# Attention's second pass three steps ahead at a change of head, and its products two steps behind in the projection

## The chip, the cores and the metric

The kernel runs on one core of a Trainium2 chip. The metric is the device time of one execution in microseconds (us): 2467.56 is the median of three runs of the kernel before (2466.41 to 2468.1). The engines are TensorE (PE, with its weight loads as PEld), VectorE (DVE), ScalarE (ACT), GpSimd (POOL) and SyncE (SP); transfers are issued from SP's and POOL's queues.

## The reference

One layer works on x of 2048 tokens by 1024 columns. A normed input is projected by w_in; three mixers share the result; their outputs are projected by w_out and added; then comes a feed-forward of 4096 hidden columns, and a last norm.

```python
def _layer(x, ...):
    p = _rmsnorm(x, g_attn) @ w_in
    # mixer a: y_a = a_b * conv3(a_c * a_h)
    # mixer b: GLU, causal conv of width 31, layer norm, silu
    # mixer c: stick-breaking attention, 8 heads of 64:
        z = q @ k.T / sqrt(64)
        mask = s_idx < t_idx
        log_beta = log_sigmoid(z)
        log_1m = where(mask, log_beta - z, 0.0)
        suffix = cumsum(log_1m, reverse=True) - log_1m
        a = where(mask, exp(log_beta + suffix), 0.0)
        o = a @ v
    x = x + concat([y_a, y_b, y_c]) @ w_out
    return x + square(relu(_rmsnorm(x, g_ffn) @ w_ff1)) @ w_ff2
```

The weight a of a key is its own sigmoid times the product of (1 - sigmoid) over the keys behind it up to the query. The kernel computes these products directly, with sigmoids and multiplications, from the last key to the first.

## The kernel before

All large products are made of three: each operand is split into a high and a low part, and hi x hi, lo x hi and hi x lo are summed (L103, L105, L107 in one helper). A split is a copy on ScalarE (L88, the high part) and a subtraction (L90, the low part) on VectorE or GpSimd.

The program has two stages. In the **projection** (to about 515 us), `p_half` makes tiles ps_p of 128 x 512, each of 24 products. Beside it, as side generators, run the mixers (mixer b is 30 multiply-adds on VectorE per tile, L450), the splitting of weights for later (`pre_split`), and attention for the first quarter of the queries. Then come four **blocks** of 512 tokens (`block(tb)`, tb = 0 to 3). Each makes the out-projection (ps_x2 in the program's text, ps_x in the profile), the first feed-forward product (ps_u, then ScalarE and VectorE make fh and fl, L899) and the second (ps_y, added to acc at L924). Their weights come as w<-s_w_out and w<-s_w over SP's queue. Attention for quarters 1, 2 and 3 of the queries runs beside blocks 0, 1 and 2.

Attention goes in 32 groups (h, i): head h, quarter i, in the order i = 0 with heads 0 to 7, then i = 1 and so on. They are called heads 0 to 31 here. A group does this:

- `a_load`: the queries and the keys of its own quarter into KQd, two transfers on POOL's queue. KQd has one buffer, so the load can't start before the last product that reads it, of the head ahead.
- `a_pass1`: 3 + 4i steps. Each makes one tile ps_z of logits (L513, L514), sigmoids A and om or R, and the running products (A*R on GpSimd L593, R on VectorE L595). Steps 0 to 2 treat the diagonal part, the others the earlier keys Kl, which are loaded behind KQd.
- `a_cross_a`: the running product across the partitions, on VectorE: a transpose to T (L606), a scan to O (L609), the factors C (L617) and T again (L623). It is made twice where i > 0, once after step 2 and once at the end.
- `a_pass2`: 3 + 4i steps. Each multiplies A by ps_q (the factors transposed, L641; L644 for the first three steps, L651 for the others), splits it (Ahi at L88 on ScalarE, Alo at L90 on GpSimd) and makes the products with the values into ps_o (L682 for the first three steps with Vd, L690 and L691 for the others with Vl). The products of a step are issued a few steps later, as the entry `late` says.

`attention` runs pass 1 of one head and pass 2 of the head ahead in alternation, by counting the steps done, d1 of n1 and d2 of n2. The load for the next head is placed after both are through. A side generator is advanced by `weave`: it is to have done so much of its cost when the main work has come so far. The sizes of the buffer rings stand in `self.ab`, one for the projection (pool at1), one for the blocks (pool at2).

The order on each engine is not that of the text alone: the framework's scheduler, with its own simulated time, arranges the instructions. What each engine has in its list stands fixed from then on, and it works it off in order.

Of the kernel before, what the change touches and what calls it, by code (L numbers as in the profile page):

```python
# [68 lines left out]
class Trunk:  # L69
# [195 lines left out]
    def norm_spread(self, g):  # L265
        self.R[g] = self.mx.tile([P, TB], F32, name="R", tag="Rs", bufs=4)
        self.nc.scalar.activation(self.R[g], self.spread(self.rv[g], "o" if g else "q"), AF.Copy)

# [54 lines left out]
    def p_evac(self, hf, u, sub, tb, ps):  # L323
# [4 lines left out]
        kind = UNITS[u]  # L328
        R = self.R[gtb]
        sig, ca = self.sig, self.ca  # L330
# [206 lines left out]
    def a_pass1(self, g):  # L537
        nc, pool, i = self.nc, self.at, g["i"]
        ab = self.ab
        lo, hi2 = slice(0, 256), slice(256, 512)  # L540

        def new(name, bufs, shape=(P, TB), dt=F32):
            return pool.tile(list(shape), dt, name=name, tag=name, bufs=bufs)

        if i:
            g["Kl"] = pool.tile([P, self.kmax], F32R, name="Kl", tag="Kl", bufs=self.ab["Kl"])
            for rows, kq in self.kq_halves(g["h"]):
                to = g["Kl"][rows, : TB * i].rearrange("c (j q) -> c j q", j=2)
                self.load_r(to, kq[:, 0, :, : TB * i // 2])
        A0 = g["A0"] = []  # L550
        Rd = new("Rd", 1)

        k2 = [g["Kd"][:, 0:P], g["Kd"][:, 256 : 256 + P]]
        z = self.a_z(g, [(k2[1], lo, lo), (k2[0], lo, hi2)])
        t, om = self.a_diag(z, 0)
        nc.gpsimd.tensor_tensor(t[:, hi2], t[:, hi2], om[:, lo], op=ALU.mult)
        nc.vector.tensor_tensor(Rd[:, lo], om[:, lo], om[:, hi2], op=ALU.mult)
        A0.append(t)
        yield 1

        k4 = self.every(g["Kd"], 4)
        z = self.a_z(g, [(k4[3], hi2, lo), (k4[2], hi2, hi2)])
        t, om = self.a_diag(z, 1)
        nc.gpsimd.tensor_tensor(t[:, hi2], t[:, hi2], om[:, lo], op=ALU.mult)
        R = new("R", 2)
        nc.vector.tensor_tensor(R[:, lo], om[:, lo], om[:, hi2], op=ALU.mult)
        A0.append(t)
        yield 1
        z = self.a_z(g, [(k4[1], hi2, lo), (k4[0], hi2, hi2)])
        t, om = self.a_diag(z, 2)  # L570
        nc.vector.tensor_tensor(R[:, hi2], om[:, lo], R[:, lo], op=ALU.mult)
        nc.gpsimd.tensor_tensor(t, t, R, op=ALU.mult)
        nc.vector.tensor_tensor(Rd[:, hi2], om[:, hi2], R[:, hi2], op=ALU.mult)
        A0.append(t)
        yield 1
        tot = self.a_cross_a(g, Rd, None)
        if not i:
            return
        J = 4 * i
        kl = self.every(g["Kl"][:, : TB * i], J)  # L580
        full = slice(0, TB)
        R = None
        for j in range(J - 1, -1, -1):
            z = self.a_z(g, [(kl[j], full, full)])
            t = new("A0", ab["A0"])
            if R is None:
                nc.scalar.activation(t, z, AF.Sigmoid, scale=0.125)
                R = new("R", 2)
                nc.scalar.activation(R, z, AF.Sigmoid, scale=-0.125)
            else:  # L590
                nc.scalar.activation(t, z, AF.Sigmoid, scale=0.125)  # L591
                nc.scalar.activation(z, z, AF.Sigmoid, scale=-0.125)  # L592
                nc.gpsimd.tensor_tensor(t, t, R, op=ALU.mult)  # L593
                Rn = new("R", 2)
                nc.vector.tensor_tensor(Rn, z, R, op=ALU.mult)  # L595
                R = Rn
            A0.append(t)
            yield 1
        self.a_cross_a(g, R, tot)
# [93 lines left out]
    def attention(self, groups):  # L693
        prev = None
        nxt = self.a_load(*groups[0])
        for n in range(len(groups) + 1):
            g, nxt = nxt, None
            p1 = self.a_pass1(g) if g else iter(())
            p2 = self.a_pass2(prev) if prev else iter(())
            n1 = 3 + 4 * g["i"] if g else 0  # L700
            n2 = 3 + 4 * prev["i"] if prev else 0
            d1 = d2 = 0.0
            live1, live2 = g is not None, prev is not None
            loaded = False
            while live1 or live2:
                if live2 and (not live1 or d2 * max(n1, 1) <= d1 * max(n2, 1)):
                    try:
                        next(p2)
                        d2 += 1
                        yield 0.5  # L710
                    except StopIteration:
                        live2 = False
                elif live1:
                    try:
                        next(p1)
                        d1 += 1
                        yield 0.5
                    except StopIteration:
                        live1 = False
                if not loaded and self.ab["KQd"] > 1 and d1 >= n1 / 2 and n + 1 < len(groups):  # L720
                    nxt = self.a_load(*groups[n + 1])
                    loaded = True
            if not loaded and n + 1 < len(groups):
                nxt = self.a_load(*groups[n + 1])
            prev = g
# [269 lines left out]
    def build(self):  # L995
        tc = self.tc
        with ExitStack() as ctx:
            self.consts(ctx)
            self.attention_consts(ctx)
            self.raw = ctx.enter_context(tc.tile_pool(name="raw", bufs=1))  # L1000
            self.xb = 5
            self.presplit = [("w_out", c, q) for c in range(DC) for q in range(2)] + [("w1", c, q) for c in range(PRE) for q in range(2)]
            self.g, self.u, self.w, self.R, self.rv, self.sig, self.ca, self.ss, self.yraw = ({} for _ in range(9))
            with ExitStack() as c1:
                self.psum_pool(c1, d=3, c=1, z=2, q=1, o=1)
                self.p_pools(c1)
                self.w_eng = "dve"
                self.sb = 2
                self.xl = [[None] * DC for _ in range(2)]
                self.xh = [[None] * DC for _ in range(2)]  # L1010
                with tc.tile_pool(name="raw0", bufs=1) as self.rp:
                    self.rb, self.rt = 21, "raw"
                    self.p_start()
                self.rp = self.raw
                self.rb, self.rt = self.xb, "xt"
                self.at = c1.enter_context(tc.tile_pool(name="at1", bufs=1))
                self.ab = dict(KQd=1, Kl=1, A0=5, om=2, Alo=2, Ahi=2, Vl=1, late=1, yc=2)
                weave(self.p_half(0), [(Side(self.mixer_b(0)), 83, 20, 225, True), (Side(self.x_norms()), 24, 60, 180, True)])
                self.heads = {}
                a0 = Side(self.attention([(h, 0) for h in range(H)]))  # L1020
                weave(self.p_half(1), [(Side(self.mixer_b(1)), 90, 0, 190, True), (a0, 28, 0, 210, True), (Side(self.pre_split()), len(self.presplit), 0, 200, True)])
            with ExitStack() as c2:
                self.psum_pool(c2, d=3, z=3, q=1, o=1)
                self.at = c2.enter_context(tc.tile_pool(name="at2", bufs=1, reuse_waits="tile"))
                self.st = c2.enter_context(tc.tile_pool(name="st2", bufs=1, reuse_waits="tile"))
                self.ha = c2.enter_context(tc.tile_pool(name="ha", bufs=1, reuse_waits="tile"))
                self.hp = c2.enter_context(tc.tile_pool(name="hp", bufs=1, reuse_waits="tile"))
                self.ob = 2
                self.kmax = 1536
                self.ab = dict(KQd=1, Kl=1, A0=15, om=2, Alo=3, Ahi=3, Vl=2, late=2, yc=1)  # L1030
                at = Side(self.attention([(h, i) for i in (1, 2, 3) for h in range(H)]))
                self.heads = {}

                def attend(i):
                    while self.heads.get(i, 0) < H:
                        at.advance(at.done + 1)

                self.attend = attend
                self.end = iter(())
                for tb in range(4):  # L1040
                    weave(self.block(tb, self.end), [(at, (74, 95, 107)[tb], 45, 365 if tb < 2 else 320, False)] if tb < 3 else [])
# [48 lines left out]
```

## Time and profile before

| | us |
|---|---|
| median of three runs | 2467.56 (2466.41 to 2468.1) |
| profiled execution | 2472.6 |
| its span | 2470.9 |
| mean granted clock of TensorE | 0.988 |
| TensorE busy | 2399.2 (97%) |
| VectorE busy | 1605.9 (65%) |
| GpSimd busy | 1135.1 (46%) |
| ScalarE busy | 1033.8 (42%) |

The times come from runs without a profile; the profile is one execution more. A row of the timeline gives the start, the duration, the engine, line and operation, out<-in with the count, and in brackets how long the engine was idle ahead of it and what released it. A row of waits gives who waited for whom: the total, how often, the longest. The clock is the share of full speed that TensorE was granted.

### The profile page before, as it was taken

The numbers are of one execution on the slowest core, as the hardware profiler recorded it, in microseconds if no ns is written. First come the engines' busy times: TensorE is split into PE (matmuls) and PEld (weight loads), VectorE is DVE, ScalarE is ACT, GpSimd is POOL, SyncE is SP. The second block draws the span as 40 slices with busy tenths as digits, with TensorE's granted clock in tenths as the row PEclk, the third lists the DMA queues.
The fourth block names the chain that finished last, engine by engine and source line by source line (L and its number), as shares of the span: only waits on it lengthen the run. The fifth ranks groups of instructions, "written<-read, shape, count | busy, mean of one in ns | idle before, by whom it ended". The sixth has DMA issues, their size and how long they took to land.

```text
span 2470.9 us, 32483 instructions
## 1 busy us (share of the span) xinstructions
PE 2399.2 (97%) x11316; PEld 2017.4 (82%) x11316; DVE 1605.9 (65%) x2372; ACT 1033.8 (42%) x1910; POOL 1135.1 (46%) x1197
## 2 busy tenths in 40 slices
PE   8999989997999999999999999999999999999998
PEld 7888878896778878778888888888888888888887
DVE  7958698934688878867677768676666735212114
ACT  5233432223556656535455555345555532121121
POOL 1343246633376666635566667257888730000000
PEclk9999999998999999999999999999999999999999
DMA  7579997766778987787787777776666655655555
GB/s 260 191 263 305 303 299 188 233 204 221 214 208 238 224 242 208 183 236 262 252 228 249 234 230 210 238 243 178 188 195 198 199 191 203 245 194 187 202 181 188
DMA packets 237156, 550.62 MB, mean 223 GB/s; under 512 B 26048, under 2 KB 99776, under 8 KB 218560
## 3 DMA queue, kind: packets, MB, share of 16 engines
q1 hardware_dynamic: 180912, 474.07, 56.3%
q0 software_dynamic: 53888, 73.42, 15.6%
q8 instruction: 90, 1.47, 0.2%
q10 hardware_dynamic: 2192, 1.05, 0.1%
q14 instruction: 74, 0.61, 0.1%
HBM read 391.17 MB, written 148.90 MB: 219 GB/s over the span
## 4 chain that ended last, share of the span: by engine, by line
PE 74%; DVE 12%; DMA 9%; issue 3%; POOL 1%; ACT 1%; SPq 0%; POOLq 0%; DVEq 0%; ACTq 0%
PE ps_y L103 8%; PE ps_y L107 8%; PE ps_y L105 8%; PE ps_u L103 8%; PE ps_u L105 8%; PE ps_u L107 8%; PE ps_p L105 3%; PE ps_p L103 3%; PE ps_p L107 3%; DMA KQd<-KQ 2%; PE ps_z L513 2%; DMA w<-s_w 2%; PE ps_z L514 2%; PE ps_x L105 2%; DVE ps_c L450 2%
## 5 line engine op out<-in xcount | busy, mean ns | idle before, releaser
L90 POOL TENSOR_TENSOR Alo<-A,Ahi 128x512 fp32r<-128x512 f32 x288 | 398.8, 1397 | 112.1 <-ACT Ahi L88 44.5
L924 DVE TENSOR_TENSOR acc<-acc,ps_y 128x512 f32<-128x512 f32 (+1 forms) x264 | 174.7, 665 | 179.6 <-PE ps_y L107 178.2
L103 PE MATMUL ps_y<-fh,w 128*128 128x512 f32 (+1 forms) x1056 | 283.3, 386 | 7.3 <-DVE acc L924 4.3
L103 PE MATMUL ps_u<-hh,w 128*128 128x512 f32 x1024 | 277.6, 392 | 6.1 <-DMA w<-s_w 6.1
L105 PE MATMUL ps_y<-fh,w 128*128 128x512 f32 (+1 forms) x1056 | 279.5, 384 | 0.0
L107 PE MATMUL ps_y<-fl,w 128*128 128x512 f32 (+1 forms) x1056 | 278.7, 384 | 0.2 <-DVE fl L899 0.2
L107 PE MATMUL ps_u<-hl,w 128*128 128x512 f32 x1024 | 276.1, 390 | 0.0
L105 PE MATMUL ps_u<-hh,w 128*128 128x512 f32 x1024 | 275.3, 390 | 0.0
L593 POOL TENSOR_TENSOR A<-A,R 128x512 f32<-128x512 f32 x168 | 230.9, 1377 | 93.2 <-ACT A L591 73.5
L889 ACT ACTIVATE ps_u<-ps_u 128x512 f32<-128x512 f32 x128 | 74.6, 583 | 459.7 <-PE ps_u L107 459.6
L118 POOL TENSOR_TENSOR rs_y<-rs_v,mhalf 128x4 f32<-128x4 f32 (+1 forms) x13 | 14.3, 1097 | 513.1 <-DVE rs_v L117 453.6
L103 PEld LDWEIGHTS ps_y<-fh,w 128*128 128x128 f32 x1056 | 193.6, 188 | 46.6 <-DVE acc L924 3.8
L105 PEld LDWEIGHTS ps_y<-fh,w 128*128 128x128 f32 x1056 | 195.6, 189 | 40.1
L107 PEld LDWEIGHTS ps_y<-fl,w 128*128 128x128 f32 x1056 | 195.4, 188 | 39.8 <-DVE fl L899 0.6
L103 PEld LDWEIGHTS ps_u<-hh,w 128*128 128x128 f32 x1024 | 190.4, 188 | 45.3 <-DMA w<-s_w 8.0
L105 PEld LDWEIGHTS ps_u<-hh,w 128*128 128x128 f32 x1024 | 192.2, 188 | 40.7
L107 PEld LDWEIGHTS ps_u<-hl,w 128*128 128x128 f32 x1024 | 192.5, 188 | 40.0
L88 ACT ACTIVATE Ahi<-A 128x512 fp32r<-128x512 f32 x288 | 177.1, 629 | 97.3 <-PE ps_o L690 54.2
L899 DVE TENSOR_TENSOR fl<-ps_u,fh 128x512 fp32r<-128x512 f32 x128 | 87.6, 685 | 191.3 <-ACT fh L898 190.9
L595 DVE TENSOR_TENSOR R<-ps_z,R 128x512 f32<-128x512 f32 x168 | 115.4, 687 | 140.8 <-ACT ps_z L592 99.9
L450 DVE SCALAR_TENSOR_TENSOR ps_c<-g,wb,ps_c 128x512 f32<-128x512 f32 x240 | 179.9, 750 | 4.7
L90 DVE TENSOR_TENSOR w<-wraw,w 128x512 fp32r<-128x512 f32 x152 | 143.4, 962 | 36.1 <-ACT w L88 35.5
(171 smaller groups left out, 4850.5 us busy)
## 6 DMA issues: line engine op xcount, KB each, us to landing
w<-s_w SPq DMA_DIRECT2D x200, 512.0 KB, 3.5
w<-s_w SPq DMA_DIRECT2D x68, 1024.0 KB, 4.8
wraw<-in_w SPq DMA_DIRECT2D x192, 256.0 KB, 5.1
w<-s_w_out SPq DMA_DIRECT2D x64, 512.0 KB, 4.7
s_w<-w SPq DMA_DIRECT2D x32, 1024.0 KB, 6.0
s_w<-w SPq DMA_DIRECT2D x56, 512.0 KB, 4.9
KQd<-KQ POOLq DMA_DIRECT2D x64, 384.0 KB, 7.0
xraw<-in_xT SPq DMA_DIRECT2D x48, 256.0 KB, 4.8
```

The costliest lines, as they stand in the source:

```text
L88: nc.scalar.activation(hi, x, AF.Copy)
L90: e.tensor_tensor(lo, x, f(hi), op=ALU.subtract)
L103: self.nc.tensor.matmul(ps, wh, xh, start=start and k == 0, stop=False)
L105: self.nc.tensor.matmul(ps, wl, xh, start=False, stop=False)
L107: self.nc.tensor.matmul(ps, wh, xl, start=False, stop=stop and k == n - 1)
L450: nc.vector.scalar_tensor_tensor(t, g[:, k : k + TB], self.wb[:, c, k : k + 1], t, op0=ALU.mult, op1=ALU.add)
L513: nc.tensor.matmul(z[:, oc], keys, g["qh"][:, qc], start=k == 0, stop=False)
L593: nc.gpsimd.tensor_tensor(t, t, R, op=ALU.mult)
L595: nc.vector.tensor_tensor(Rn, z, R, op=ALU.mult)
L889: nc.scalar.activation(ps, ps, AF.Relu)
L899: nc.vector.tensor_tensor(lo, ps, f(hi), op=ALU.subtract)
L924: nc.vector.tensor_tensor(acc[d][:, cols], acc[d][:, cols], ps, op=ALU.add)
```

## The change

In the projection's `self.ab`, Alo and Ahi get three buffers instead of two, `late` is 2 instead of 1, and R has one buffer instead of two (a new entry, which only step 1 of pass 1 reads; the blocks keep two). In `attention`, pass 2 of the head ahead may go on while its steps less two are not ahead of pass 1's share, so that three of its steps instead of one come before the first step of pass 1. This holds only where the head ahead has i > 0; the others go as before.

```diff
-        R = new("R", 2)
+        R = new("R", ab["R"])
...
+            lead = 2 if prev and prev["i"] else 0
             loaded = False
             while live1 or live2:
-                if live2 and (not live1 or d2 * max(n1, 1) <= d1 * max(n2, 1)):
+                if live2 and (not live1 or (d2 - lead) * max(n1, 1) <= d1 * max(n2, 1)):
...
-                self.ab = dict(KQd=1, Kl=1, A0=5, om=2, Alo=2, Ahi=2, Vl=1, late=1, yc=2)
+                self.ab = dict(KQd=1, Kl=1, A0=5, om=2, R=1, Alo=3, Ahi=3, Vl=1, late=2, yc=2)
...
-                self.ab = dict(KQd=1, Kl=1, A0=15, om=2, Alo=3, Ahi=3, Vl=2, late=2, yc=1)
+                self.ab = dict(KQd=1, Kl=1, A0=15, om=2, R=2, Alo=3, Ahi=3, Vl=2, late=2, yc=1)
```

In the changed file the lines below `attention` have numbers higher by two.

The scheduler turns this into other orders. On TensorE in the projection, the four products of head 1's first pass-2 step (Vd_3005) stand among those of one ps_p tile. Before:

```order
L103 MATMUL ps_p<-xh_5_2462,wh_2785 128x512
L682 MATMUL ps_o<-Ahi,Vd_3005 128x256
L103 MATMUL ps_p<-xh_6_2468,wh_2785 128x512
L103 MATMUL ps_p<-xh_7_2474,wh_2785 128x512
L105 MATMUL ps_p<-xh_0_2432,wl_2784 128x512
L105 MATMUL ps_p<-xh_1_2438,wl_2784 128x512
L105 MATMUL ps_p<-xh_2_2444,wl_2784 128x512
L682 MATMUL ps_o<-Alo,Vd_3005 128x256
L682 MATMUL ps_o<-Ahi,Vd_3005 128x256
L682 MATMUL ps_o<-Alo,Vd_3005 128x256
```

And in the changed kernel, at the end of the same tile:

```order
L107 MATMUL ps_p<-xl_6_2469,wh_2781 128x512
L107 MATMUL ps_p<-xl_7_2475,wh_2781 128x512
L682 MATMUL ps_o<-Ahi,Vd_3005 128x256
L682 MATMUL ps_o<-Alo,Vd_3005 128x256
L682 MATMUL ps_o<-Ahi,Vd_3005 128x256
L682 MATMUL ps_o<-Alo,Vd_3005 128x256
L513 MATMUL ps_z<-KQd 128x256
```

The first of the four has moved behind 18 products of the tile, and all four stand together.

On VectorE in the out-projection of block 1 (acc is its sum, ss the sum of squares, ot the output of block 0), before:

```order
L793 TENSOR_TENSOR ss<-ss,sq 128x512
L595 TENSOR_TENSOR R<-ps_z,R 128x512
L606 STREAM_TRANSPOSE T<-R 128x16x32
L609 SCALAR_TENSOR_TENSOR O<-T,d_90 128x528
L617 TENSOR_TENSOR C<-C,O 32x16 x3
L623 TENSOR_TENSOR T<-O,C 128x16x32
L849 TENSOR_TENSOR acc_10428<-ps_x_10400,xt 128x512
L641 STREAM_TRANSPOSE ps_q<-T 128x512
L991 SCALAR_TENSOR_TENSOR ot<-acc_5674,g_final,ps_R 128x512
L651 TENSOR_TENSOR A_9912<-A_9912,ps_q 128x512
```

And now, at the same sum:

```order
L795 TENSOR_TENSOR ss<-ss,sq 128x512
L595 TENSOR_TENSOR R<-ps_z,R 128x512
L851 TENSOR_TENSOR acc_10426<-ps_x_10398,xt 128x512
L993 SCALAR_TENSOR_TENSOR ot<-acc_5674,g_final,ps_R 128x512
L857 SCALAR_TENSOR_TENSOR hl<-acc_10426,g_ffn,hh 128x512
L795 TENSOR_TENSOR ss<-ss,sq 128x512
L851 TENSOR_TENSOR acc_10469<-ps_x_10441,xt 128x512
```

The whole cross step of head 17 and the products with ps_q behind it have left the out-projection; they stand in the ps_u stage that follows.

On GpSimd, at the load of the keys of head 13 in block 0, before:

```order
L83 DMA Vd_7830<-VS 128x512
L90 TENSOR_TENSOR Alo<-A_7276,Ahi 128x512
L593 TENSOR_TENSOR A_7681<-A_7681,R 128x512
L90 TENSOR_TENSOR Alo<-A_7306,Ahi 128x512
L593 TENSOR_TENSOR A_7697<-A_7697,R 128x512
L83 DMA KQd<-KQ 64x6x256 x2
L83 DMA Kl<-KQ 64x2x256 x2
L90 TENSOR_TENSOR Alo<-A_7408,Ahi 128x512
L593 TENSOR_TENSOR A_7756<-A_7756,R 128x512
L83 DMA Vl<-VS 128x512
```

And now:

```order
L593 TENSOR_TENSOR A_7695<-A_7695,R 128x512
L90 TENSOR_TENSOR Alo<-A_7460,Ahi 128x512
L83 DMA Vl<-VS 128x512
L90 TENSOR_TENSOR Alo<-A_7512,Ahi 128x512
L90 TENSOR_TENSOR Alo<-A_7604,Ahi 128x512
L593 TENSOR_TENSOR A_7756<-A_7756,R 128x512
L83 DMA KQd<-KQ 64x6x256 x2
L83 DMA Kl<-KQ 64x2x256 x2
L593 TENSOR_TENSOR A_7808<-A_7808,R 128x512
L83 DMA Vd_8249<-VS 128x256
```

The load Vl of the values, which stood behind the keys, stands ahead of them, and the Vd for head 13's own second pass follow at once (those for head 12's, Vd_7830 among them, stand ahead in both orders).

## The prediction

> **What bounds the kernel now.** I read the page's first part, then the list of waits on TensorE, then the windows round its largest gaps, and last the timeline at the passages that the change moves.
>
> ```profile
> span 2470.9 us, 32483 instructions
> PE 2399.2 (97%) x11316; PEld 2017.4 (82%) x11316; DVE 1605.9 (65%) x2372; ACT 1033.8 (42%) x1910; POOL 1135.1 (46%) x1197
> ```
>
> TensorE is busy 2399.2 of 2470.9 us, and the change adds or removes no product. So the time can move only by the 71.7 us in which TensorE is idle, and by slow-clock time inside the busy part. The waits (total, times, longest) say where the idle time lies:
>
> ```profile
> PE ps_z L513 <- DMA KQd<-KQ: 13.6, 9, 2.9
> PE ps_x L103 <- ACT y L88: 9.1, 1, 9.1
> PE ps_o L682 <- ACT Ahi L88: 6.5, 2, 5.6
> PE ps_u L103 <- DMA w<-s_w: 6.1, 8, 1.9
> PE ps_y L103 <- DVE acc L924: 4.3, 4, 2.3
> PE ps_x L103 <- DVE A L651: 3.9, 1, 3.9
> PE ps_y L103 <- DVE fl L899: 2.9, 2, 2.2
> ```
>
> Three of them touch what the change moves: the one wait of a projection product on its split (L682, 5.6), the one in an out-projection (ps_x, 3.9) and the waits for a head's keys (KQd). The windows round them (the stretch and its length, busy time and instructions of TensorE, its weight loads, VectorE, ScalarE and GpSimd, then granted clock, DMA share, GB/s) show the clock:
>
> ```profile
> 316.00:384.00 68.00, 59.55 (x275) 49.29 (x276) 67.31 (x103) 21.60 (x42) 39.23 (x43) 0.95 0.87 293
> 327.00:342.00 15.00, 9.40 (x41) 7.60 (x40) 14.81 (x26) 5.52 (x13) 7.93 (x10) 0.77 0.76 283
> 900.00:920.00 20.00, 17.10 (x75) 13.94 (x74) 15.36 (x23) 11.04 (x21) 12.33 (x16) 0.91 1.25 293
> 1098.00:1112.00 14.00, 10.46 (x36) 8.45 (x37) 10.42 (x16) 5.49 (x10) 7.21 (x5) 0.76 0.79 262
> 1238.00:1250.00 12.00, 9.33 (x44) 7.96 (x44) 9.68 (x16) 4.99 (x10) 5.96 (x9) 0.86 1.00 260
> 1555.00:1612.00 57.00, 57.00 (x264) 47.60 (x263) 31.83 (x47) 20.25 (x35) 16.41 (x15) 1.00 0.81 265
> ```
>
> A gap is paid twice: 15 x (1 - 0.77) = 3.4 us round the 5.6 us gap and 14 x (1 - 0.76) = 3.4 us round the 3.9 us gap are lost to a lower clock, and 20 x 0.09 = 1.8 and 12 x 0.14 = 1.7 us round the two longest key waits.
>
> **A, two steps behind in the projection.** No instruction is added; the four products of Vd_3005 (head 1, k = 0) stand 18 projection products later. Eight such products take 1.81 us on the chain, so 18 x 0.227 = 4.1 us.
>
> ```profile
> 49.67 1.81 PE ps_p L103 x8
> 335.43 0.58 PE L682 MATMUL ps_o<-Ahi,Vd 128*128 128x256 f32 x1 [5.60 <-ACT Ahi L88]
> 345.29 1.67 POOL L361 TENSOR_TENSOR ca<-ca,R 128x512 f32<-128x512 f32 x1 [2.96 <-DVE ca L360]
> 346.91 1.36 POOL L83 DMA_DIRECT2D KQd<-KQ  x2
> 356.42 0.36 PE L513 MATMUL ps_z<-KQd 128*128 128x256 f32 x1 [2.07 <-issue]
> 394.11 0.35 PE L513 MATMUL ps_z<-KQd 128*128 128x256 f32 x1 [0.15 <-DMA KQd<-KQ]
> ```
>
> Most of 5.6 + 3.4 = 9.0 us vanishes at 335 us. But it is not the end of that account. VectorE is busy 67.31 of the 68 us from 316 to 384: that stretch is its work. The keys of head 3 are issued at 346.91 behind the mixer's L361 on GpSimd's queue, which waited for VectorE's L360; they come when VectorE lets them, and TensorE meets them at 356.42, where it waits already. What it saves at 335 it would wait again at 356 or at 394. I price A at 0. Upper bound: all of it kept, -9.0. Lower bound: a short wait at 356 or 394 grows by what is saved and far enough that the clock falls there too, as it did after the key wait in 1238 to 1250: +1.7. One buffer of R instead of two costs nothing: with i = 0 a head writes R once, and the next head's write comes a passage later (37 us between the two z rows above). The third Alo and Ahi make no instruction either; they only loosen GpSimd's L90.
>
> **B, the out-projection of block 1.** Before, the last z of head 17 and with it the load of head 18's keys fall in the ps_x stage:
>
> ```profile
> 1086.79 1.36 POOL L83 DMA_DIRECT2D KQd<-KQ  x2 [3.88 <-PE ps_o L682]
> 1088.14 1.21 POOL L83 DMA_DIRECT2D Kl<-KQ  x2
> 1091.57 0.32 SPq L79 DMA_DIRECT2D w<-s_w_out  x1
> 1101.54 1.19 PE L103 MATMUL ps_x<-y,w 128*128 128x512 f32 x2 [3.88 <-DVE A L651]
> ```
>
> The trace's name for this wait is VectorE's L651, but the weights asked for at 1091.57 had only landed at about 1101.4: the DMA view of 1086 to 1093 gives this load 9.8 us, the page 4.7 for all 64 of its kind.
>
> ```profile
> w<-s_w_out SPq DMA_DIRECT2D x3, 512.0 KB, 9.8
> KQd<-KQ POOLq DMA_DIRECT2D x2, 384.0 KB, 8.3
> Kl<-KQ POOLq DMA_DIRECT2D x2, 256.0 KB, 12.0
> w<-s_w_out SPq DMA_DIRECT2D x64, 512.0 KB, 4.7
> ```
>
> So about 2 x 384 + 2 x 256 + 256 KB of head loads went beside the weights. In the changed order two pass-2 steps come ahead of that last z, and since attention is advanced by the blocks' own progress, the last z falls behind the out-projection: between the sums of block 1 VectorE's order has no transpose, scan, C, or product with ps_q left, and GpSimd's no KQd. Block 2's out-projection, which has no passage, shows the result: 57.00 of 57.00 us busy (1555 to 1612). I take the whole 3.9 + 3.4 = -7.3; the other bound is 0, if the weights stay late for another cause.
>
> By the Trainium skill ("DMA: Bandwidth & Descriptors", Issuing engines are not separate DMA queues), transfers started by sync and by GpSimd end on the same 16 engines and interleave. The 9.8 against 4.7 us agrees; the rule speaks against the change as well, since the moved load is not gone but meets ffn1's weights (a rival below).
>
> **C, the passages in the blocks.** KQd has one buffer, so the load of a head's keys cannot be issued before the last z of the head ahead, and TensorE must fill the time till they land:
>
> ```profile
> DMA to landing us min/median/max: 4.5/7.0/13.4
> 900.90 9.90 DMA KQd<-KQ
> 910.93 0.36 PE L513 MATMUL ps_z<-KQd 128*128 128x256 f32 x1 [2.90 <-DMA KQd<-KQ]
> 1229.88 13.37 DMA KQd<-KQ
> 1243.38 0.55 PE L513 MATMUL ps_z<-KQd 128*128 128x256 f32 x1 [2.67 <-DMA KQd<-KQ]
> PE ps_z L513 <- DMA KQd<-KQ: 7.1, 5, 2.9
> PE ps_z L513 <- DMA KQd<-KQ: 2.7, 1, 2.7
> ```
>
> The last two rows are the list of waits cut to 600 to 1060 and to 1112 to 2060 us: 9.8 of the 13.6 us lie in the blocks.
>
> One would think that two more pass-2 steps ahead of the first z make this cover longer. Counted in both orders they do not. Over heads 9 to 31 (without 18 and 26) 46.8 products stand between last and first z before, 47.5 after: 46.8 x 0.227 = 10.6 and 10.8 us, because the two steps led are taken from the same place, behind the last z of the head ahead. Only the spread moves: head 11 goes from 9.5 to 14.0 us, head 13 from 11.1 to 7.9. Setting the time from last z to landing that each head had in this trace against the new covers gives 14.1 us of waits where the old covers give 9.8, and three slow-clock windows (3 x 1.7) for two: +6. But which load is slow depends on what runs beside it, and that moves too; by the equal mean alone it is 0. I take +3, the middle, as neither bound has a row nearer. The new pass-2 products need no load: the order puts Vd 25 to 40 rows of GpSimd ahead of them.
>
> The Trainium skill ("TensorE: Matmul & The Clock Gate", Part 1) has the clock halve only after an idle window of about 3.4 us. The rows differ: gaps of 2.67 and 2.90 us came with 0.86 and 0.91. By the page the clock's part of C would be nothing and its upper bound +4; I keep the rows.
>
> **D, VectorE's bursts in the blocks.**
>
> ```profile
> 996.28 7.68 DVE L609 TENSOR_TENSOR_SCAN O<-T,d 128x528 f32<-128x528 f32 x1
> 1012.20 0.96 PE L103 MATMUL ps_y<-fh,w 128*128 128x512 f32 x3 [2.27 <-DVE acc L924]
> 1710.17 1.64 PE L103 MATMUL ps_y<-fh,w 128*128 128x512 f32 x4 [2.23 <-DVE fl L899]
> ```
>
> At head 17 a scan of 7.68 us and the products with ps_q behind it hold up acc, and TensorE waits at 1012. The lead splits such bursts at some passages and joins them at others. The two rows' waits, with L924's 4.3 and L899's 2.9 in all and the clock's 1.7, bound it at about -4 and, mirrored, +4; I take -1.
>
> **Sum:** 0 - 7.3 + 3 - 1 = -5.3 us. The profiled execution took 2472.6 us with a span of 2470.9; it lies 5.0 above the median of the runs, 2467.56. So the profiled execution should come to 2467.3, and the median to 2467.56 - 5.3 = 2462.3; I say 2462.
>
> **The rivals.**
>
> Gain kept in the projection: VectorE's list between 316 and 384 us is not the bound all the way, and its order may put the mixer's row ahead of head 1's, so that the keys go out earlier. For it: GpSimd is busy only 39.23 of these 68 us, so it would issue them at once. Against it: VectorE's 67.31 of 68. Then -9.0 more: 2453.
>
> No change: B is gained, and the passages take it back by the +6 above and a burst of D in the wrong place (+1): 2467.56 - 7.3 + 7 = 2467.
>
> Slower, through one mechanism: GpSimd's queue in front of the keys. In the new order Vl's load stands four rows ahead of KQd where it stood behind it, and two Alo splits and a product A*R of the same size precede it, a split taking 1.4 us by the page's row:
>
> ```profile
> L90 POOL TENSOR_TENSOR Alo<-A,Ahi 128x512 fp32r<-128x512 f32 x288 | 398.8, 1397 | 112.1 <-ACT Ahi L88 44.5
> ```
>
> If a row like that is still running when the last z is done, the key lands 1.4 us later at each passage. With all needs 1 us longer the new covers give 22.2 us of waits, with 2 us 35.0; at 1.5 us some 28.6 and five clock windows, 8.5, together 37 against 13.2 now: +24. Less B's 7.3 that is +17: 2484. It decides from about 0.5 us per passage. Against it: most covers still exceed the median load of 7.0, and Vl ahead of the keys has usually left when they go.
>
> Collision moved, not removed: head 18's keys now go beside ffn1's weights, whose waits (L103 ps_u, 6.1 in 8, at most 1.9) show that this stream has little slack. Then a gap like the old one stands in ffn1 and B gives 0: 2467.56 + 2 = 2470.
>
> That the change does not do what it says is excluded for the order; for TensorE it may be so in A, which is priced.
>
> **How the numbers follow.** Less than about 0.2% (4.9 us) can't be told from no change. The forecast has 0.42, the gain kept 0.16, no change 0.18, the queue 0.14, the moved collision 0.10. The forecast's own range is 2457 to 2467 (C's 0 to +6 and D); its middle lies just under 2462.6, where faster begins, and something over half of it counts as faster: 0.24, with the gain kept 0.40, and 0.06 of the others, where B comes whole and C at its lower bound: 0.46. The queue and half the collision are slower, 0.20 with a burst in a wrong place; the rest, 0.34, is the same. The range 2450 to 2480 takes in the gain kept with B whole and all but the worse half of the queue.
>
> **What would show it.** In the changed kernel's profile: ps_x L103 <- DVE A L651 gone, and the out-projection of block 1 all busy (B). L682 <- Ahi gone, but the z waits at heads 3 and 4 longer by about as much, and VectorE still 99% busy there (A). KQd waits of 14 to 19 us instead of 13.6 (C). The prediction is wrong if KQd's waits pass 25 us, if the time that TensorE idles between 316 and 400 us falls by over 5 us, or if the ps_u waits grow past 10.

## The result and the profile after

The changed kernel took 2483.61 us (median of six runs, 2478.88 to 2494.12) against 2467.83 us for the kernel before: 1.0068 of its time, with a 95% interval of 1.0048 to 1.0087. It is slower by 16 us between the medians, 17 by the ratio. The prediction said 2462 us, in a range of 2450 to 2480: the sign was wrong, and the time lies outside the range.

The profiled execution of the changed kernel, 2478.88 us, is the shortest of its six, while the one of before, 2472.6 us, was above its median. So these two traces show 6.2 us of span between them; the change's execution lies 4.7 us below its median and the one of before 4.8 above, which makes up the rest. What follows is read from several profiles of each order, and the sizes of effects from the timed runs.

The first part of the page, after:

```profile
span 2477.1 us, 32467 instructions
PE 2398.6 (97%) x11316; PEld 2011.5 (81%) x11316; DVE 1596.3 (64%) x2372; ACT 1034.9 (42%) x1910; POOL 1124.0 (45%) x1197
```

TensorE has the same 11316 products and the same busy time (2398.6 for 2399.2); its idle time rose from 71.7 to 78.5 us. The list of TensorE's waits, after:

```profile
PE ps_z L513 <- DMA KQd<-KQ: 12.5, 11, 1.7
PE ps_u L103 <- DMA w<-s_w: 10.5, 9, 2.8
PE ps_o L682 <- ACT Ahi L88: 6.0, 3, 3.3
PE ps_y L107 <- DVE fl L901: 5.5, 3, 3.1
PE ps_z L513 <- ACT A L528: 3.9, 2, 2.3
PE ps_y L103 <- DVE acc L926: 2.2, 2, 2.0
PE ps_y L103 <- DVE fl L901: 1.8, 1, 1.8
```

Beside the list of before one sees: the wait in the out-projection (ps_x on L651, 3.9) is gone, as forecast. The keys (KQd) are as they were, 12.5 for 13.6. But the first feed-forward product (called ffn1 in the prediction) now waits 10.5 us for its weights where it waited 6.1, fl (L901, both rows) 7.3 where it was 3.1, and the projection's split (L682 on Ahi) still 6.0 where it was 6.5.

The growth of the weights' waits is in block 1. Before, from 1100 to 1562 us:

```profile
PE ps_u L103 <- DMA w<-s_w: 0.9, 3, 0.6
PE ps_z L513 <- DMA KQd<-KQ: 2.7, 1, 2.7
```

And the same stretch after:

```profile
PE ps_u L103 <- DMA w<-s_w: 7.6, 5, 2.8
PE ps_z L513 <- DMA KQd<-KQ: 4.1, 3, 1.5
PE ps_y L103 <- DVE acc L926: 2.2, 2, 2.0
```

The lengths of the stages, from the first product of one to the first of the next, tell the same. Columns: before, the projection's part alone (e1 below), the change, the change once more (e3), the lead alone (e2).

| stage, us | before | e1 | change | e3 | e2 |
|---|---|---|---|---|---|
| projection | 575.4 | 576.5 | 574.3 | 574.9 | 573.3 |
| block 0, feed-forward | 431.7 | 435.5 | 425.7 | 426.6 | 427.7 |
| block 1, out-projection | 57.8 | 57.0 | 49.2 | 49.1 | 49.6 |
| block 1, feed-forward | 439.3 | 438.9 | 455.7 | 456.4 | 459.2 |
| block 2, feed-forward | 450.4 | 451.2 | 457.6 | 456.6 | 456.5 |

With the lead (last three columns), block 1's out-projection is 8 us shorter, of which 11 products fewer make 2.5. Its feed-forward is 16 to 20 us longer, of which 13 products more make 2.9. Block 2 loses 6 to 7. The gain that the forecast rests on is there, some 6 of the 7.3 us, and the stage behind it gives back more than twice as much. These differences stand clear of the scatter: over five profiles with the order of before in block 1 its two stages take 493.7 to 497.1 us together, over four with the changed order 504.9 to 508.8; for block 2's feed-forward it is 449.2 to 451.2 and 456.5 to 457.6.

### The profile page after: what moved, and what is told of

It is laid out like the page before. It is cut to its first block, busy times and chain, and to the rows that moved or that the text cites. A ratio compares the mean times of both kernels' runs of the same rounds, so it can differ in the third digit from the quotient of the medians.

```text
span 2477.1 us, 32467 instructions
## 1 busy us (share of the span) xinstructions
PE 2398.6 (97%) x11316; PEld 2011.5 (81%) x11316; DVE 1596.3 (64%) x2372; ACT 1034.9 (42%) x1910; POOL 1124.0 (45%) x1197
## 4 chain that ended last, share of the span: by engine, by line
PE 62%; DVE 16%; DMA 12%; issue 4%; POOL 3%; ACT 2%; SPq 1%; DVEq 0%; POOLq 0%; ACTq 0%
PE ps_y L107 8%; PE ps_y L103 8%; PE ps_y L105 8%; PE ps_u L103 7%; PE ps_u L107 7%; PE ps_u L105 7%; DVE ps_c L450 5%; DMA KQd<-KQ 3%; DMA w<-s_w 2%; PE ps_x L105 2%; PE ps_x L107 2%; PE ps_z L513 2%; PE ps_x L103 2%; PE ps_z L514 2%; DMA xraw<-in_xT 2%
## 5 line engine op out<-in xcount | busy, mean ns | idle before, releaser
L103 PE MATMUL ps_u<-hh,w 128*128 128x512 f32 x1024 | 279.3, 393 | 10.5 <-DMA w<-s_w 10.5
L926 DVE TENSOR_TENSOR acc<-acc,ps_y 128x512 f32<-128x512 f32 (+1 forms) x264 | 175.0, 665 | 172.8 <-PE ps_y L107 171.4
L593 POOL TENSOR_TENSOR A<-A,R 128x512 f32<-128x512 f32 x168 | 225.9, 1351 | 116.3 <-ACT A L591 88.1
L901 DVE TENSOR_TENSOR fl<-ps_u,fh 128x512 fp32r<-128x512 f32 x128 | 87.4, 683 | 209.5 <-ACT fh L900 209.3
L595 DVE TENSOR_TENSOR R<-ps_z,R 128x512 f32<-128x512 f32 x168 | 115.4, 687 | 108.2 <-ACT ps_z L592 76.4
```

Source lines behind the costliest of these rows:

```text
L103: self.nc.tensor.matmul(ps, wh, xh, start=start and k == 0, stop=False)
L901: nc.vector.tensor_tensor(lo, ps, f(hi), op=ALU.subtract)
L926: nc.vector.tensor_tensor(acc[d][:, cols], acc[d][:, cols], ps, op=ALU.add)
```

## The experiments

Orders are fixed when a kernel is built, so two kernels can be compared instruction by instruction: in e1 every engine has the order of before in the blocks; in e2 that of before in the projection and that of the change in the blocks; e5 to e7 have TensorE's order of the change in one block and of before in the others, but for a few rows at the borders. So these parts can be told apart. e4, e8, e9 and e15, which split a tile, have an order of their own in the projection too.

**e1, the projection's part alone.** The change with

```diff
-            lead = 2 if prev and prev["i"] else 0
+            lead = 0
```

> The projection's part alone (late 2, three Alo and Ahi, one R); in the blocks every engine has the order of before. Theory P (the lead in the blocks costs all of it, the projection's part is held by VectorE): 2465 to 2469, within 0.1% of before. Rival Q (the projection's part does harm that goes on into the blocks): at least +5, 2473 or more. Rival R (its gain is kept and the lead costs still more): 2459 to 2463.

Measured: 2472.86 us against 2467.48, ratio 1.0015 (1.0001 to 1.0028): some 3.7 us slower. No theory had this: P and R fall, Q has the sign but is too large. In its trace no stage of blocks 1 and 2 is longer than before's by more than 0.8 us; of its 5.0 us more in span, 1.1 are in the projection and 3.8 in block 0's feed-forward, which has the order of before.

**e2, the lead alone.** Before, with the changed `attention`.

> The lead of two steps alone; the projection has the order of before, the blocks that of the change. Theory P: 2481 to 2486, as the whole change. Rival Q: about half of it, 2473 to 2477. Rival R: 2486 to 2491.

Measured: 2480.19 us, ratio 1.0056 (1.0036 to 1.0076), +13.8 us. That is the greater part of the change's 16.8. P's range misses by 1 us; that the lead costs most of it stands.

**e3, the changed kernel again.**

> The changed kernel once more, for a second profile and more times: 2479 to 2494, median about 2484. If the scatter (15 us where before has 6) comes from waits for keys and weights at the passages, the profile has these in other sizes than the first (12.5 for the keys, 10.5 for ffn1's weights) and their sum goes with the time; if it comes from VectorE's bursts, these two stay and L901 and L926 change.

Measured: 2485.26 us (2480.68 to 2491.85), ratio 1.0068 (1.0048 to 1.0089). Its profile has 17.6 us of waits for keys where the first had 12.5, and 10.4 for the weights where it had 10.5; L901 goes from 7.3 to 5.4, L926 from 2.2 to 2.4. So the late weights are there in both, and the keys' waits change most from one execution to the next. But this execution took only 1.8 us more than the first, 2480.68 us: what the slower ones wait for, up to 2494, neither profile shows.

**e4, the queries in two buffers.** The change, with KQd split in two tiles, and room made in A0:

```diff
+        t = pool.tile([P, 1, TB], F32R, name="KQd", tag="Kd", bufs=1)
+        u = pool.tile([P, 2, TB], F32R, name="KQq", tag="KQd", bufs=self.ab["KQd"])
...
-                self.ab = dict(KQd=1, Kl=1, A0=15, om=2, R=2, ...
+                self.ab = dict(KQd=2, Kl=1, A0=13, om=2, R=2, ...
```

> The change, with the keys and queries of a head in two tiles, the queries (qh, ql) with two buffers in the blocks, so that a head's load goes out in the middle of the pass ahead and not behind its last z; A0 has 13 buffers for 15 to make room. If the late keys are what costs (theory K), the KQd waits of 12.5 us fall under 3 and the time to 2462 to 2470. If it is the collision of transfers with ffn1's weights or VectorE's bursts (theory W), the keys' waits go and the time stays above 2476.

Measured: 2469.83 us, ratio 1.0001 (0.9988 to 1.0015). The change, timed beside it, took 2485.26 (e3): 15.4 us are back. The longest waits in blocks 0 to 2 (600 to 2062 us) of this kernel, whose line numbers are higher by two more:

```profile
PE ps_u L103 <- DMA w<-s_w: 10.0, 7, 3.0
PE ps_y L103 <- DVE acc L928: 5.7, 4, 3.3
PE ps_y L107 <- DVE fl L903: 3.4, 2, 3.1
PE ps_y L103 <- DVE fl L903: 1.1, 2, 0.8
```

Waits for keys are gone from these blocks; the waits for ffn1's weights are not. So the keys' waits and these are two things, and what the lead costs can be made up at the first. This doesn't yet say that the lead made the keys worse: before waited as long for them. The order moves with the split and the second buffer as well, in the projection too, where the queries keep one buffer.

**e5, e6, e7, the lead in one block at a time.** The lead alone, with

```diff
-            lead = 2 if prev and prev["i"] else 0
+            lead = 2 if prev and prev["i"] == 1 else 0    # e5; 2 in e6, 3 in e7
```

> The lead only where the head ahead has i = 1: block 0 in the order of the change, the projection and blocks 1 and 2 in that of before. Theory L (each block has its own balance, read from the stages of the six profiles so far: block 0's ffn stage shorter by 5 to 7 us): 2460 to 2463, faster than before by 0.2 to 0.3%. Rival S (every passage with a lead costs about the same, 12.7 us over three blocks): 2470 to 2473.

> The lead only where the head ahead has i = 2: block 1 in the order of the change, the rest in that of before. Theory L (out-projection of block 1 shorter by the 7.3 us of its gap, its ffn stage longer by 15 us through waits for w<-s_w, 8 where it had 1, and for keys): 2474 to 2479. Rival S: 2470 to 2473. Rival B (the gap's gain is kept, as forecast): 2458 to 2463.

> The lead only where the head ahead has i = 3: block 2 in the order of the change, the rest in that of before. Theory L (VectorE's late fl and R and the key waits in block 2, +5 us in the stages): 2471 to 2475. Rival S: 2470 to 2473. Its profile tells them apart in one thing: by L the waits are on VectorE and ScalarE (L901, L528, L595), some 6 us where before has 2.2.

Measured against 2466.42 us: e5 2464.34, ratio 0.9992 (0.9978 to 1.0006); e6 2479.38, 1.0049 (1.0031 to 1.0068); e7 2475.38, 1.0038 (1.0021 to 1.0055). So the lead is worth nothing that can be told in block 0, costs 12 us in block 1 and 9 in block 2. The waits are those that L names: in e6's block 1 the weights w<-s_w take 7.1 us where before has 0.9, and in e7's block 2 L901, L528 and L595 take 7.5 where before has 2.2. Rival S falls with e5 and B with e6. L gave the order of the three right; the gain that it saw in block 0 is not there: e5's own block 0 took 434.9 us, longer than before's 431.7, with the order that took 425.7 to 427.7 in three other profiles (and 431.8 in e11, below). That stage scatters by more than the effect. The three sum to 19 us where e2 measures 13.8; each of the four has an interval of 3.5 to 5 us to either side.

**e11 and e12, block 1 without its stores.** In block 1 the split second weights are stored for the later blocks (s_w<-w, 1 MB each). These two kernels, the lead alone and the kernel before, leave the stores out; blocks 2 and 3 split the raw weights again.

```diff
-        first = -1 if (name, *at) in self.presplit else {"w_out": 0, "w1": 0, "w2": 1}[name]
+        first = -1 if (name, *at) in self.presplit else {"w_out": 0, "w1": 0, "w2": 4}[name]
```

> The lead alone, but block 1 does not store the split w2 (32 transfers of 1 MB); blocks 2 and 3 split it anew from the raw weights instead, so their time is other and only block 1 is read. If ffn1's late weights in block 1 come from too many transfers at once: the ps_u waits on w<-s_w fall from 8 to 9 us to under 3 and block 1's out-projection and ffn stage together from 505 to 509 us to under 500. If they come from the order alone: they stay within 2 us.

> The kernel before with the same left out: the control to the run ahead. Transfers as the cause: the gap of 3.9 us in block 1's out-projection goes too, the two stages fall from 497 us to 490 to 493, and the lead's kernel comes within 4 us of it there. Order as the cause: the lead's kernel stays 8 us or more behind it.

Whole times are of no use here (2487.33 and 2491.05 us, more work in block 2). Waits from 1100 to 1560 us, the lead alone (e2):

```profile
PE ps_u L103 <- DMA w<-s_w: 7.6, 7, 3.1
PE ps_z L513 <- DMA KQd<-KQ: 5.7, 1, 5.7
PE ps_y L103 <- DVE acc L926: 2.4, 2, 2.0
```

and the same stretch without the stores (e11):

```profile
PE ps_z L513 <- DMA KQd<-KQ: 3.3, 2, 2.9
PE ps_y L103 <- DVE acc L926: 0.9, 2, 0.7
PE ps_u L103 <- DVE Rd L557: 0.5, 1, 0.5
```

The waits for the split weights are gone, and the out-projection and feed-forward of block 1 take 494.3 us where the lead alone had 508.8. Without the stores the kernel before takes 491.7 there (497.1 with them): the lead is 2.6 us behind it, where it was 11.7. So the transfers are what makes block 1 lose, by one profile of each kernel. One point missed: the control's gap in the out-projection did not go (3.2 us at the longest). No store of split weights runs there in either kernel; the head's load does, as in before, and where the lead moves that load the gap is gone. The scheduler also moved some rows in block 1 when the stores went; that part is not separated.

**e8, e9, e15, where the lead is wanted with early keys.** e8 is e4 with the projection's settings of before; e9 has the lead for i = 1 and 3 only, e15 for i = 3 only (there the 13 buffers of A0 are laid out for it).

> The lead with the queries in two buffers and A0 in 13, and the projection in the order of before. If the projection's part costs what e1 shows (+5 between the medians, +3.7 by the ratio): 2463 to 2466. If that was chance: 2468 to 2471.

> The projection of before, the queries in two buffers, A0 in 13, the lead where the head ahead has i = 1 or 3, none in block 1. If block 1 loses by the lead itself (transfers bunched in its ffn stage): its three stages fall from e8's 551 us to 545 to 548 and the time to 2457 to 2461, faster than before by 0.2 to 0.4%. If block 1's loss is only the late keys, which the second buffer has taken away already: 2462 to 2465 as e8.

> e9 without the lead in block 0 (the lead stays where i = 3, as A0 has 13 buffers). If the second buffer is the whole gain of e9 and the lead is worth nothing in block 0: within 2 us of e9, 0.2 to 0.35% faster than before. If the lead gains in block 0 once the keys are early: 4 to 6 us behind e9, 0 to 0.15% faster than before.

Measured: e8 2463.55 us, ratio 0.9991 (0.9977 to 1.0006); e9 2461.80, 0.9969 (0.9955 to 0.9984); e15 2457.72, 0.9960 (0.9944 to 0.9975). Each is compared with the kernel before as timed beside it. By the ratios e8 is 2.5 us ahead of e4, by the medians against before 5.2: the same sign as e1's 3.7, but the intervals overlap. Block 1's three stages (its own two and the out-projection of block 2) are 551.1 us in e8, 554.4 in e9 and 548.5 in e15: e9's gain is not where it was expected, in block 1; its profile has it in the projection and block 0, where its order is that of e8, so this is no effect of the edit. e15, with the lead left out in both blocks, is the fastest, and faster than both kernels of the diff: the lead adds nothing that can be told in blocks 0 and 1.

That the second buffer is the whole gain is not shown. The split of the tile changes the projection as well: with their common order there, e8, e9 and e15 come to the first product of the out-projection at 567.2 to 569.9 us (mean 568.3), the nine profiles with the order of before at 569.6 to 575.7 (mean 573.1). That is nearly half of the 10 us by which e15 is ahead. No kernel has the split without the second buffer, or both without any lead.

**e10, three buffers but one step behind.** e1 with `late=1`.

> The projection with three Alo and Ahi and one R, but its products one step behind as before; blocks as before. If the two steps behind cost what the projection's part costs: 2465 to 2468, one wait of about 5.6 us at L682, none at 374 us. If the one buffer of R or the other order on GpSimd costs it: 2471 to 2474.

Measured: 2468.21 us against 2469.08, ratio 0.9995 (0.9977 to 1.0013), and no wait at 374 us; the longest wait at L682 is 3.4 us at 335, shorter than expected. So no cost of the buffers and R can be told, and the 3.7 us of e1 go best with the two steps behind. The intervals of e1 and e10 overlap, so this is likely and not shown.

**e13 and e14, VectorE and GpSimd in block 2.** e7, and the kernel before, with three low parts per head of block 2 made on VectorE:

```diff
-            self.split(hi, lo, t, "pool")
+            self.split(hi, lo, t, "dve" if i == 3 and k < 3 else "pool")
```

What is behind it is seen in e7's timeline at the passage to head 28:

```profile
1755.02 6.87 DVE L557 TENSOR_TENSOR Rd<-om 128x256 f32<-128x256 f32 x1
1757.10 2.56 POOL L90 TENSOR_TENSOR Alo<-A,Ahi 128x512 fp32r<-128x512 f32 x2
1759.63 0.73 POOL L564 TENSOR_TENSOR A<-A,om 128x256 f32<-128x256 f32 x1
1760.32 1.28 POOL L90 TENSOR_TENSOR Alo<-A,Ahi 128x512 fp32r<-128x512 f32 x1
1763.15 0.61 PE L513 MATMUL ps_z<-KQd,Kl 128*128 128x512 f32 x1 [2.30 <-ACT A L528]
1767.93 0.51 PE L103 MATMUL ps_y<-fh,w 128*128 128x512 f32 x1 [1.79 <-DVE fl L901]
```

A product Rd that takes 0.40 us at its shortest is busy for 6.87 us, while GpSimd works off pass 2's splits beside it, and it ends (1761.89) just behind the last of them (1761.60). ScalarE, then TensorE at 1763, then fl and TensorE at 1768 wait for it. The change has 11 such products Rd and R of over 2.5 us in the blocks, 44.6 us together; before has 2, 7.4 us.

> e7 (lead in block 2 alone) with the low parts of the first three pass-2 steps of i = 3 made on VectorE, not on GpSimd. If GpSimd's work beside them stretches VectorE's Rd and R: no such product over 2.5 us in block 2 (e7 has four, 22.5 us together), the waits for L528 and fl (7 us in e7) under 3, block 2's ffn stage 450 to 453 for e7's 456.7 and the time 2468 to 2471. If the order costs it by itself: stage 456 or more, since VectorE has three splits more per head; 2475 or more.

> The kernel before with the same three splits on VectorE, the control to e13: block 2's ffn stage within 2 us of before's 450.4 and the time within 3 us of before, as nothing waits for VectorE there but 2.2 us.

Measured: e13 2471.22 us, ratio 1.0006 (0.9992 to 1.0019); its block 2 feed-forward took 451.0 us, 5.7 less than e7's 456.7, and the waits at L528 are gone, those for fl at 1.0. That supports the theory against the order alone, as far as one profile goes: the scheduler moved rows of TensorE in block 2 as well. But three products of over 2.5 us remain in block 2 (11.1 us for e7's 22.5), and e14 goes against its expectation: 2472.41 us, 1.0014 (0.9998 to 1.0029), block 2 at 457.6, with one wait of 6.5 us for fl behind an R of 7.53 us. Whether such a product costs anything depends on who needs VectorE just then: e15 has 11 of them in its blocks (38.0 us) and is the fastest of all.

Nor are Rd and R the only ones. The scan of the cross step (its shortest, median and longest time in ns stand behind the count) shows it in the kernel before:

```profile
L609 DVE TENSOR_TENSOR_SCAN O<-T,d x56: 1229/1496/7682, 240.5 to 1977.3; 128x528 f32<-128x528 f32 x56
```

and in the change:

```profile
L609 DVE TENSOR_TENSOR_SCAN O<-T,d x56: 1236/1490/3223, 240.8 to 1987.0; 128x528 f32<-128x528 f32 x56
```

Before has eight scans of over 2.5 us in the blocks, 31.5 us together, the change one, 3.2. With Rd and R that is 38.9 us before and 47.8 after, while VectorE's whole busy time fell (1605.9 to 1596.3). So the lead moved this stretching from the scans to the first products of a new head, on which its next steps wait, more than it added to it. That this is what block 2 pays for is argued from the waits at L528, L595 and fl, and e13 and e14 pull apart on it.

## Why the prediction was wrong, point by point

**A, the projection.** The mechanism held: what is saved at 335 us is waited for again, with VectorE busy all through. The step that failed is the place of the new wait. The forecast put it at the keys, at 356 or 394; it is at the next head's own products. The change's rows:

```profile
335.36 0.39 PE L682 MATMUL ps_o<-Ahi,Vd 128*128 128x256 f32 x1 [2.28 <-ACT Ahi L88]
336.72 0.39 PE L682 MATMUL ps_o<-Alo,Vd 128*128 128x256 f32 x1 [0.97 <-POOL Alo L90]
373.71 0.38 PE L682 MATMUL ps_o<-Ahi,Vd 128*128 128x256 f32 x1 [3.29 <-ACT Ahi L88]
375.06 0.38 PE L682 MATMUL ps_o<-Alo,Vd 128*128 128x256 f32 x1 [0.97 <-POOL Alo L90]
```

The 5.60 us became 3.25, and at head 2, where before had no wait, 4.26 are new. The windows of the change show VectorE full, and a clock of 0.89 in both places:

```profile
316.00:384.00 68.00, 59.03 (x264) 48.19 (x264) 66.95 (x98) 21.73 (x41) 35.99 (x40) 0.95 0.84 271
327.00:342.00 15.00, 11.75 (x49) 9.31 (x48) 14.84 (x25) 6.91 (x14) 9.70 (x11) 0.89 0.86 297
370.00:385.00 15.00, 10.74 (x47) 8.65 (x46) 14.89 (x21) 4.44 (x8) 11.41 (x13) 0.89 0.63 187
384.00:400.00 16.00, 14.39 (x65) 10.96 (x64) 15.76 (x26) 4.08 (x9) 7.46 (x11) 1.00 1.03 246
```

In before, TensorE is busy all through the third of them, and the clock falls in the fourth:

```profile
370.00:385.00 15.00, 15.00 (x75) 12.50 (x73) 14.79 (x23) 5.58 (x10) 11.88 (x13) 1.00 0.73 229
384.00:400.00 16.00, 14.96 (x62) 11.33 (x61) 15.43 (x25) 5.74 (x12) 8.27 (x9) 0.89 0.88 173
```

So the clock takes no more from the change here than from before: 2 x 15 x 0.11 = 3.3 us against 3.4 (15 x 0.23) and 1.8 (16 x 0.11). By the start of the same ps_p product, over three profiles with the two steps and nine with the order of before, the projection is 2.9 us earlier at 347 us, 3.7 later at 392, and 2.2 later at its end. The step was priced at 0 between -9.0 and +1.7; the timed runs say +3.7 (0.2 to 6.9), and these 2.2 us are the greater part of it, as far as the scatter of single profiles (569.6 to 575.7 us at the end, in one order) allows. Its lower bound held one lost wait and not a second place with a wait of its own. That this bound was too narrow is likely and not shown, since the interval holds +1.7 as well.

**B, the out-projection of block 1.** This is the step that failed most. It was right as far as it looked: its gap (3.88 us and 3.4 us of clock) is gone in every profile with the lead in block 1. It failed in taking the gain as the end of the matter: -7.3 was forecast, and block 1 measures +12 (e6). The rows of the change behind it:

```profile
1106.49 1.17 PE L103 MATMUL ps_u<-hh,w 128*128 128x512 f32 x4 [1.37 <-DMA w<-s_w]
1119.71 1.36 POOL L83 DMA_DIRECT2D KQd<-KQ  x2 [36.92 <-PE ps_z L514]
1128.22 1.21 PE L103 MATMUL ps_u<-hh,w 128*128 128x512 f32 x4 [2.21 <-DMA w<-s_w]
1136.42 0.36 PE L513 MATMUL ps_z<-KQd 128*128 128x256 f32 x1 [1.51 <-DMA KQd<-KQ]
```

Head 18's load now goes out at 1119.71 into the first feed-forward product, where its weights, raw weights and stores run. The DMA view of 1111 to 1124 us, the change:

```profile
w<-s_w SPq DMA_DIRECT2D x5, 512.0 KB, 10.3
s_w<-w SPq DMA_DIRECT2D x1, 1024.0 KB, 10.7
KQd<-KQ POOLq DMA_DIRECT2D x2, 384.0 KB, 13.9
Kl<-KQ POOLq DMA_DIRECT2D x2, 256.0 KB, 17.7
```

The matching stretch of before, 1126 to 1139 us, as far behind the start of its feed-forward:

```profile
w<-s_w SPq DMA_DIRECT2D x5, 512.0 KB, 9.5
s_w<-w SPq DMA_DIRECT2D x1, 1024.0 KB, 11.7
```

Weights take nearly as long there, but TensorE does not wait: the first four weight transfers of the feed-forward, asked for from 1109.7 on, had landed from 4.1 us ahead of its first product to 5.8 us behind it (in the change from 1.2 ahead to 6.4 behind), and no keys were asked for behind them. The change removed none of the transfers: it let TensorE reach the same stretch earlier and put head 18's loads into it. The lead isn't needed for such a collision: e9 and e15, without it in block 1 but with the queries' load moved by the second buffer, wait 7.5 and 4.5 us for these weights, and e9 has a gap of 2.8 us in the out-projection besides. How much belongs to the earlier arrival and how much to the moved loads is not separated. The rival of the moved collision named this mechanism, with a chance of 0.10, and the sentence on the Trainium skill's "DMA: Bandwidth & Descriptors" (Issuing engines are not separate DMA queues) said why: the queues interleave on the same engines. Its price, 0 in place of -7.3, was still too low, as the late weights come again at 1300 us (2.76) and at other places. One sign that the prediction set for itself came true: the ps_u waits passed 10 us (10.5, and 10.4 in e3).

```profile
1300.29 1.32 PE L103 MATMUL ps_u<-hh,w 128*128 128x512 f32 x3 [2.76 <-DMA w<-s_w]
```

**C, the keys.** The size was about right, as far as waits go. In blocks 0 to 2 they are 11.1 us (first profile), 11.7 (e3) and 11.4 (e2) for the 9.8 of before; the forecast was +3 with the clock. The reason, equal cover on average, fits. What it did not see is that the loads themselves take a little longer in the median: 7.8, 7.6 and 7.5 us in the change, e3 and e2 for 7.3 and 7.0 in before and e1. The change's row for 600 to 2060 us:

```profile
KQd<-KQ POOLq DMA_DIRECT2D x46, 384.0 KB, 7.8
```

The rival of GpSimd's queue, which gave 2484, met the measured time by luck: Vl ahead of the keys did not bring its 28.6 us of waits for keys, but the 11 to 12 above.

**D, VectorE in the blocks.** Priced at -1 within 4 us either way; block 2 alone costs +9 (e7), 6 of it seen in its stage. The step that failed is the bound of 4 us, taken from two rows of before. The forecast looked at where bursts of A*Q and the scan of 7.68 us stand, and took that scan as it was; its shortest is 1.23 us, and six instructions of GpSimd, two of them DMA issues, ran beside it. With two more steps of pass 2 ahead of the first z, their splits on GpSimd run just when Rd and R of the new head are due (the rows at 1755 above).

**The sum.** In place of 0 - 7.3 + 3 - 1 stands, by the timed parts, +3.7 for the projection, nothing that can be told for block 0, +12 for block 1 and +9 for block 2, in all some 25 us where the whole change measures 17; the intervals of the parts, 3 to 5 us to either side each, leave room for that. What stays open is what the slower executions of the change wait for, since each of its two profiles is of the shortest of six.

## What to carry to other kernels

A gap on the bounding engine ahead of a full transfer stretch is not a gain until the transfers behind it have been counted: closing it lets the engine arrive sooner at loads that come no sooner. Where a single buffer's load can only be asked for behind its last reader, moving work about the passage shifts the wait from head to head, and a second buffer for the part that is read to the end took these waits away in the blocks (e4; e15 has none there either, with the lead in block 2 alone). In a stretch where a second engine is 99% busy, putting its consumers later moves the wait to the next consumer.

## What the runs showed of the hardware

VectorE's small products are stretched severalfold beside GpSimd's work: 0.40 to 6.87 us for the same 128x256 product. All eleven long ones of the change end 0.28 or 0.29 us behind the end of a GpSimd instruction that ran beside them, and several GpSimd instructions can pass one after another before the product gets through.

The granted clock can fall after short gaps. These are the change's rows, a wait at 1214.76 and three windows round such gaps:

```profile
1214.76 1.64 PE L103 MATMUL ps_y<-fh,w 128*128 128x512 f32 x4 [1.99 <-DVE acc L926]
1125.00:1145.00 20.00, 16.28 (x76) 12.78 (x74) 15.01 (x26) 9.15 (x18) 10.65 (x14) 1.00 0.95 179
1205.00:1225.00 20.00, 18.01 (x73) 14.53 (x72) 19.75 (x26) 6.99 (x13) 12.37 (x12) 0.91 0.51 173
1295.00:1310.00 15.00, 12.11 (x56) 10.00 (x55) 6.90 (x8) 7.91 (x16) 9.64 (x13) 0.89 0.74 223
```

A gap of 1.99 us was followed by 20 x 0.09 = 1.8 us of lost clock, one of 2.76 us by 15 x 0.11 = 1.7, while the one of 2.21 us at 1128 cost none (1125 to 1145 is at 1.00). The Trainium skill ("TensorE: Matmul & The Clock Gate", Part 1) names an idle window of about 3.4 us; here well under that was at times enough, so a wait of 2 us can cost nearly 4.
